# A two-layer network with a dense expert layer on one Trainium2 core: read-back activations in buffers of their own, and 104 instead of 96 expert columns multiplied ahead in the second layer

## Chip, cores and metric

One core of one Trainium2 chip runs the whole program, all in float32 with matrix products split in two or three parts. The metric is the device time of one execution in microseconds (us). Engines are named as in the profile: PE (matmul), PEld (PE's weight load), DVE, ACT, POOL, and SP, whose queue issues every DMA spoken of here.

## The reference, cut to what matters

Two layers over 256 context tokens and 256 latent tokens; the second layer needs the latent tokens alone. Each layer is a mixer (convolution, mLSTM and attention heads side by side) and then an expert layer with 16384 experts. The mixer is not touched by the change. The expert layer is

```python
def one(t):
    q = (t @ wq).reshape(TOKEN_BLOCK, PEER_HEADS, 2, PEER_DK // 2)
    s = jnp.einsum("thpd,hpnd->thpn", q, sub_keys).astype(jnp.float32)
    st, it = lax.top_k(s, PEER_TOPK)
    ...
    e = jnp.take_along_axis(cidx, pos, axis=-1)
    g = jax.nn.softmax(best, axis=-1)
    u = jnp.take(eu, e, axis=0)
    act = jax.nn.gelu(jnp.einsum("thkd,td->thk", u, t).astype(jnp.float32), approximate=False)
    return jnp.einsum("thk,thkd->td", (g * act).astype(ev.dtype), jnp.take(ev, e, axis=0))
```

Each of the 8 heads of a token picks 16 experts by product keys, weighs them with a softmax, and adds up `g * gelu(u . t) * v` over the chosen ones.

## The kernel before, in words

The kernel does the expert layer densely: it multiplies all 16384 experts with all tokens, and a gate matrix G that is zero for experts that were not chosen picks out the right ones. The experts lie in 128 columns `j` of 128 experts each. Layer 0 has n = 512 tokens and layer 1 has n = 256, so one 128x512 tile of activations holds one column in layer 0 and two columns in layer 1 (`per` = 1 and 2).

The expert layer of each layer (`peer`, L896) has two passes.

The **early pass** multiplies columns with the `u` weights (`inner`, L874): load `u`, split each half into a rounded part `uh` (ACT, L869) and a rest `ul` (L870, on POOL here), 24 matmuls (L887 to L889), gelu into a tile `ga` (L893), and a store of that tile to a DRAM buffer `act` (L916). These columns are interleaved with the routing: a top-k phase, and then `spread` (L806), which writes G. One step of `spread` takes four tokens: one-hot tiles on DVE (L824, L832) and ACT (L829, L830), four matmuls L836, two reductions L838 on DVE; every eight steps a 2 MB store of G (L841). The constants `RATE` say how many columns are put in per routing step, `MORE` how many between the two phases, and `NPRE` how many of the 128 columns are multiplied in the early pass at all (128 in layer 0, 96 in layer 1).

The **value pass** (`outer`, L940) then goes over all columns two at a time. `weights` (L946) loads a 1 MB piece `g` of G for every four columns (L954), reads the stored activations back from `act` (L960), multiplies the two on DVE (L966), and splits the product into `wh` (ACT, L969) and `wl` (DVE, L970). `values` (L975) loads the column's `v` (512 KB, L977) and splits both halves into `vh` (ACT, L869) and `vl` (DVE, L870). `second` multiplies: per token tile and half one matmul each of L992, L993 and L994, 24 per column in layer 0 and 12 in layer 1, each 512 wide. The columns that the early pass left (32 in layer 1) get their `u` matmuls here, interleaved with the others (L1042), with their `ul` on DVE. Beside the value pass of layer 0 runs `side`: the modulation vectors for later use, 56 loads `wa` of 512 KB (L193) with two DVE operations `wtr` each (L196), behind one load and sigmoid of the condition vector `cb` (L181 to L185).

The read-back tile of L959 is named `ga` and rotates in the same three buffers of the pool `expu` as the gelu output of L892. The pools are opened and closed in turn on the same memory; a tile in a pool that lies where an earlier pool lay waits until that one is done with. The framework's scheduler turns the loops into one fixed instruction order per engine, from these buffer counts and its own durations; the engines then wait for one another by semaphores.

Of the kernel before, what the change touches and what calls it, by code (L numbers as in the profile page):

```python
# [7 lines left out]
F32 = mybir.dt.float32  # L8
# [15 lines left out]
SPLIT = 3072.0  # L24
TG = 32
TT = 512
NPRE = (128, 96)
RATE = (((1, 3), (5, 8)), ((1, 2), (1, 1)))
UB = (5, 8)
UR = (2, 4)  # L30
VB = (5, 6)
VR = (2, 3)
SPREAD = (('ap', 'as', 'ap', 'ds'), ('as', 'ds'))
LAG = (16, 4)
HB = 4
# [14 lines left out]
class Net:  # L50
# [653 lines left out]
    def route(self, l, h, c0, Gd):  # L704
# [101 lines left out]
        def spread(tt, sT, ni, sg):  # L806

            iota = self.iotap[:, None, :].to_broadcast([128, 4, 128])
            for gq in range(128 // TG):
                stg = R("stg", [128, 128, TG])  # L810
                for t4 in range(0, TG, 4):
                    kind = SPREAD[l][(gq * TG + t4) // 4 % len(SPREAD[l])]
                    t = slice(gq * TG + t4, gq * TG + t4 + 4)
# [82 lines left out]
    def peer(self, l, P, h, c0, npre, side):  # L896
# [9 lines left out]
        with ExitStack() as rs:  # L906
# [13 lines left out]
            for phase in self.route(l, h, c0, Gd):  # L920
# [4 lines left out]
                k += 1  # L925
                a, b = RATE[l][phase]
                if k * a // b > (k - 1) * a // b:
# [12 lines left out]
    def outer(self, l, P, h, c0, npre, Gd, Ad, pool, X, S, side):  # L940
# [9 lines left out]
        def weights(n2):  # L950

            if n2 % 2 == 0:
                st["g"] = X.tile([128, n // TG, 4, TG], F32, name="g", tag="g")
                nc.sync.dma_start(st["g"], Gd[:, :, 2 * n2:2 * n2 + 4, :])  # L954
            r = []
            for m in range(2 // per):
                bank = n2 * (2 // per) + m
                if bank * per < npre:
                    a = pool.tile([128, 512], F32, name="ga", tag="ga", bufs=3)  # L959
                    nc.sync.dma_start(a, Ad[bank])  # L960
                else:
                    a = st.pop(("a", bank))
                j4 = (bank * per) % 4
                av = a.rearrange("p (j a b) -> p j a b", j=per, b=TG)
                g = st["g"][:, :, j4:j4 + per, :].rearrange("p a j b -> p j a b")
                nc.vector.tensor_mul(av, av, g)  # L966
                wh = X.tile([128, 512], F32R, name="wh", tag="wh", bufs=2 * (2 // per))
                wl = X.tile([128, 512], F32R, name="wl", tag="wl", bufs=2 * (2 // per))
                nc.scalar.activation(wh, a, AF.Copy)  # L969
                nc.vector.tensor_sub(wl, a, wh)  # L970
                for k in range(per):
                    r.append((wh[:, k * n:(k + 1) * n], wl[:, k * n:(k + 1) * n]))
            st["w", n2] = r

        def values(j):  # L975
            v = X.tile([128, D], F32, name="v", tag="v", bufs=VR[l])
            nc.sync.dma_start(v, V[:, j, :])  # L977
            return self.usplit(v, "v", X, VB[l], nc.vector)
# [68 lines left out]
        for k in range(65):  # L1047
            if k == 64:
                for _ in side:
                    pass  # L1050
                self.log_exp(self.gelu)
            if k < 64:
                n2 = seq[k]
                for j in (2 * n2, 2 * n2 + 1):
                    if j >= npre:
                        a = self.inner(l, h, c0, j, per, pool, S, nc.vector)
                        if a is not None:
                            st["a", j // per] = a
                weights(n2)
                next(side, None)  # L1060
            if k:
                second(seq[k - 1])
            next(side, None)


    def run(self):
# [4 lines left out]
        for l in range(DEPTH):  # L1071
# [14 lines left out]
            def side():  # L1086
                if l == 0:
                    cb = self.condition()
                    yield
                    for k, (ll, w) in enumerate([(0, 5)] + [(1, w) for w in range(6)]):  # L1090
                        yield from self.ada(ll, P[ll], w, cb, self.I["ada_t"][k])
            self.peer(l, P[l], h, c0, NPRE[l], side())

# [84 lines left out]
```

## Time and profile before

| what | value |
|---|---|
| time, median of 3 runs | 3087.41 us (3082.68 to 3088.37) |
| profiled execution, its time and its span | 3078.09 us and 3076.4 us |
| share of the span: PE, DVE, ACT, POOL | 95%, 68%, 46%, 35% |
| layer 0: early pass, value pass | about 454 to 1230 us, 1235 to 1972 us |
| layer 1: spread phase | about 2391 to 2612 us |
| layer 1: value pass | about 2629 to 3060 us |

The span runs from the first to the last instruction of the profiled execution; 1.7 us of its time lie outside. A share over the whole span mixes stages with different limits, so the rows below come from single stages. "Idle before" is the time that an engine stood still ahead of an instruction, with the instruction or transfer that ended it.

### The profile page before, as it was taken

What the parts mean: (1) busy time and instruction counts of PE and PEld (TensorE: products, weight loads), DVE (VectorE), ACT (ScalarE), POOL (GpSimd) and SP (SyncE); (2) the same over time, 40 slices, a digit from 0 to 9 for tenths busy, and PEclk for the clock granted to TensorE, in tenths of its full rate; (3) what the DMA queues carried; (4) which work ended last, traced back from release to release, by engine and by line L of the source; (5) the groups of instructions that cost most, each with busy time, mean ns of one, the idle gap of its engine ahead of it and who ended that gap; (6) DMA issues with size and microseconds to landing.
All of it is one profiled execution on the core that took longest, in us unless ns stands there. A gap on an engine that the chain in (4) does not pass through costs nothing.

```text
span 3076.4 us, 43429 instructions
## 1 busy us (share of the span) xinstructions
PE 2923.6 (95%) x14930; PEld 2407.8 (78%) x14930; DVE 2088.7 (68%) x4556; ACT 1428.0 (46%) x2865; POOL 1064.0 (35%) x871
## 2 busy tenths in 40 slices
PE   7899989999999999999999999888999998999998
PEld 4476578888888888777777777777689998788887
DVE  7987637875666664666666665586659889666665
ACT  4335443345666655332232233345455665455554
POOL 4334245566666664000000000153478874000000
PEclk9999999999999999999999999999999999999999
DMA  6511124345555557766766766221255876988864
GB/s 227 176 51 56 41 79 136 126 139 187 187 205 184 204 184 250 236 226 222 235 222 216 233 226 199 81 76 62 68 180 174 273 264 229 304 278 263 264 222 141
DMA packets 256717, 563.53 MB, mean 183 GB/s; under 512 B 18208, under 2 KB 119072, under 8 KB 253296
## 3 DMA queue, kind: packets, MB, share of 16 engines
q1 hardware_dynamic: 255776, 558.32, 54.0%
q8 instruction: 118, 1.93, 0.3%
q0 software_dynamic: 720, 2.43, 0.2%
q14 instruction: 103, 0.84, 0.1%
HBM read 463.16 MB, written 97.52 MB: 182 GB/s over the span
## 4 chain that ended last, share of the span: by engine, by line
PE 57%; DMA 14%; DVE 12%; issue 2%; ACT 2%; POOL 1%; SPq 0%; DVEq 0%; ACTq 0%; POOLq 0%
DMA ga<-act 11%; PE h L887 10%; PE h L888 10%; PE h L889 10%; PE acc L993 6%; PE acc L994 5%; PE acc L992 5%; PE f L836 3%; DVE vl L870 2%; DVE wl L970 1%; DVE cy L491 1%; PE f L333 1%; DMA u<-in_peer_u 1%; PE f L334 1%; PE f L335 1%
## 5 line engine op out<-in xcount | busy, mean ns | idle before, releaser
L870 POOL TENSOR_TENSOR ul<-u,uh 128x512 fp32r<-128x512 f32 x448 | 590.8, 1331 | 333.9 <-ACT uh L869 320.0
L887 PE MATMUL h<-hh,uh 128*128 128x512 f32 (+1 forms) x2048 | 693.4, 339 | 2.6 <-ACT ga L893 1.4
L889 PE MATMUL h<-hh,ul 128*128 128x512 f32 (+1 forms) x2048 | 690.5, 337 | 5.2 <-POOL ul L870 5.2
L888 PE MATMUL h<-hl,uh 128*128 128x512 f32 (+1 forms) x2048 | 691.0, 337 | 0.0
L993 PE MATMUL acc<-vl,wh 128*128 128x512 f32 x1536 | 609.4, 397 | 21.2 <-DVE vl L870 19.1
L869 ACT ACTIVATE vh<-v 128x512 fp32r<-128x512 f32 x512 | 305.6, 626 | 660.2 <-DMA v<-in_peer_v 520.8
L992 PE MATMUL acc<-vh,wh 128*128 128x512 f32 x1536 | 599.6, 390 | 6.5 <-ACT wh L969 4.5
L994 PE MATMUL acc<-vh,wl 128*128 128x512 f32 x1536 | 599.9, 391 | 0.2
L869 ACT ACTIVATE uh<-u 128x512 fp32r<-128x512 f32 x512 | 319.4, 629 | 487.1 <-PE h L888 362.6
L870 DVE TENSOR_TENSOR vl<-v,vh 128x512 fp32r<-128x512 f32 x512 | 343.9, 686 | 179.5 <-ACT vh L869 178.7
L889 PEld LDWEIGHTS h<-hh,ul 128*128 128x128 f32 x2048 | 390.7, 191 | 46.4 <-POOL ul L870 5.6
L887 PEld LDWEIGHTS h<-hh,uh 128*128 128x128 f32 x2048 | 391.1, 191 | 43.6 <-ACT ga L893 2.8
L888 PEld LDWEIGHTS h<-hl,uh 128*128 128x128 f32 x2048 | 391.0, 191 | 37.2
L838 DVE TENSOR_REDUCE rt_stg<-f 128x256 f32<-128x512 f32 x384 | 244.8, 686 | 224.3 <-PE f L836 223.5
L993 PEld LDWEIGHTS acc<-vl,wh 128*128 128x128 f32 x1536 | 288.5, 188 | 113.0 <-DVE vl L870 55.5
L992 PEld LDWEIGHTS acc<-vh,wh 128*128 128x128 f32 x1536 | 288.8, 188 | 68.4 <-ACT wh L969 4.9
L994 PEld LDWEIGHTS acc<-vh,wl 128*128 128x128 f32 x1536 | 288.9, 188 | 58.9 <-DVE wl L970 1.6
L241 POOL TENSOR_TENSOR wlo<-wt,whi 128x512 fp32r<-128x512 f32 x164 | 240.7, 1479 | 247.7 <-ACT whi L240 221.7
L966 DVE TENSOR_TENSOR ga<-ga,g 128x512 f32<-128x512 f32 x192 | 131.8, 691 | 217.7 <-DMA ga<-act 201.3
L398 POOL MEMSET up<- 128x60 f32 (+1 forms) x2 | 0.3, 148 | 765.4 <-PE acc L1014 765.4
L824 DVE SCALAR_TENSOR_TENSOR rt_oh_g<-iotap,rt_sT,rt_sg 128x256 fp32r<-128x256 f32 x512 | 213.2, 474 | 0.1
L240 ACT ACTIVATE whi<-wt 128x512 fp32r<-128x512 f32 x164 | 100.5, 627 | 162.4 <-PE f L320 71.2
(317 smaller groups left out, 4277.5 us busy)
## 6 DMA issues: line engine op xcount, KB each, us to landing
u<-in_peer_u SPq DMA_DIRECT2D x256, 512.0 KB, 3.9
v<-in_peer_v SPq DMA_DIRECT2D x256, 512.0 KB, 4.7
G<-rt_stg SPq DMA_DIRECT2D x24, 2048.0 KB, 7.1
act<-ga SPq DMA_DIRECT2D x176, 256.0 KB, 2.9
ga<-act SPq DMA_DIRECT2D x176, 256.0 KB, 4.6
g<-G SPq DMA_DIRECT2D x32, 1024.0 KB, 6.0
wa<-in_ada_t SPq DMA_DIRECT2D x56, 512.0 KB, 5.6
w<-in_ada_w SPq DMA_DIRECT2D x20, 1024.0 KB, 6.3
```

The costliest lines, as they stand in the source:

```text
L241: nc.gpsimd.tensor_sub(lo, raw, hi)
L824: nc.vector.scalar_tensor_tensor(og[:, k], self.iotap[:, None, :].to_broadcast([128, 2, 128]), sT[:, 1, c:c + 1], sg[:, c, :, None].bitcas ...
L838: nc.vector.tensor_reduce(stg[:, :, t4 + k2:t4 + k2 + 2].rearrange("p j t -> p t j"), pg.rearrange("p (t x j) -> p t j x", t=2, x=2), axis ...
L869: nc.scalar.activation(hi, raw[:, k * 512:(k + 1) * 512], AF.Copy)
L870: lo_eng.tensor_sub(lo, raw[:, k * 512:(k + 1) * 512], hi)
L887: nc.tensor.matmul(o, uh, hh[:, c, c0:], start=c == 0, stop=False)
L888: nc.tensor.matmul(o, uh, hl[:, c, c0:], start=False, stop=False)
L889: nc.tensor.matmul(o, ul, hh[:, c, c0:], start=False, stop=c == NB - 1)
L966: nc.vector.tensor_mul(av, av, g)
L992: nc.tensor.matmul(A, wh[:, t], vh, start=s0, stop=False)
L993: nc.tensor.matmul(A, wh[:, t], vl, start=False, stop=False)
L994: nc.tensor.matmul(A, wl[:, t], vh, start=False, stop=s1)
```

## The change

The read-back gets a tile `gb` of its own, in the pool `X` of the value pass, with six buffers in layer 0 and four in layer 1; the three `ga` buffers stay for the gelu output and for the end of the layer. In layer 1, 104 columns are multiplied in the early pass, and nine are put in per eight spread steps where it was one per step; 24 columns are left to the value pass. All lines behind the constants move by one, so L960 becomes L961 and so on.

```diff
-NPRE = (128, 96)
-RATE = (((1, 3), (5, 8)), ((1, 2), (1, 1)))
+NPRE = (128, 104)
+RATE = (((1, 3), (5, 8)), ((1, 2), (9, 8)))
 UB = (5, 8)
 UR = (2, 4)
 VB = (5, 6)
 VR = (2, 3)
+AB = (6, 4)
...
                 if bank * per < npre:
-                    a = pool.tile([128, 512], F32, name="ga", tag="ga", bufs=3)
+                    a = X.tile([128, 512], F32, name="gb", tag="gb", bufs=AB[l])
                     nc.sync.dma_start(a, Ad[bank])
```

How the fixed order moves, at three places. The number behind a name tells one tile from the next.

**The steady part of layer 0's value pass, on DVE.** Before, from the split `wl_13380` on (`ga_13547` uses the buffer that `wl_13380` reads last, `ga_13554` the one that `wl_13463` reads last):

```order
L970 TENSOR_TENSOR wl_13380<-ga_13376,wh_13379 128x512
L196 SCALAR_TENSOR_TENSOR wtr_13383,red_13008<-wa_13365,cb_11572 128x1024
L196 SCALAR_TENSOR_TENSOR wtr_13455,red_13008<-wa_13453,cb_11572 128x1024
L870 TENSOR_TENSOR vl_13478<-v_13475,vh_13477 128x512
L966 TENSOR_TENSOR ga_13547<-ga_13547,g_13457 128x512
L870 TENSOR_TENSOR vl_13482<-v_13475,vh_13481 128x512
L970 TENSOR_TENSOR wl_13463<-ga_13459,wh_13462 128x512
L870 TENSOR_TENSOR vl_13512<-v_13509,vh_13511 128x512
L966 TENSOR_TENSOR ga_13554<-ga_13554,g_13457 128x512
L870 TENSOR_TENSOR vl_13516<-v_13509,vh_13515 128x512
```

The same place with the change (`gb_14086` uses the buffer that `wl_13824` reads last, `gb_14093` the one that `wl_13831` reads last):

```order
L971 TENSOR_TENSOR wl_13824<-gb_13820,wh_13823 128x512
L871 TENSOR_TENSOR vl_13873<-v_13870,vh_13872 128x512
L967 TENSOR_TENSOR gb_14086<-gb_14086,g_13996 128x512
L871 TENSOR_TENSOR vl_13877<-v_13870,vh_13876 128x512
L971 TENSOR_TENSOR wl_13831<-gb_13827,wh_13830 128x512
L197 SCALAR_TENSOR_TENSOR wtr_13834,red_13725<-wa_13814,cb_11572 128x1024
L197 SCALAR_TENSOR_TENSOR wtr_13906,red_13725<-wa_13904,cb_11572 128x1024
L871 TENSOR_TENSOR vl_13927<-v_13924,vh_13926 128x512
L967 TENSOR_TENSOR gb_14093<-gb_14093,g_13996 128x512
L871 TENSOR_TENSOR vl_13931<-v_13924,vh_13930 128x512
```

The multiplication by `g` now stands six tiles ahead of its own split instead of about three, and still two to six DVE rows behind the split that gives its buffer free, with the second `vl` half of a column right behind it.

**The same stretch on SP.** Before, between two loads of `g`:

```order
L954 DMA g_13635<-G0_3117 128x16x128
L977 DMA v_13419<-in_peer_v 128x1024
L193 DMA wa_13453<-in_ada_t 128x1024
L960 DMA ga_13459<-act0_3118 128x512
L960 DMA ga_13466<-act0_3118 128x512
L977 DMA v_13475<-in_peer_v 128x1024
L977 DMA v_13509<-in_peer_v 128x1024
L960 DMA ga_13547<-act0_3118 128x512
L193 DMA wa_13543<-in_ada_t 128x1024
L977 DMA v_13563<-in_peer_v 128x1024
L960 DMA ga_13554<-act0_3118 128x512
L954 DMA g_13818<-G0_3117 128x16x128
```

With the change:

```order
L955 DMA g_13635<-G0_3117 128x16x128
L978 DMA v_13297<-in_peer_v 128x1024
L961 DMA gb_13459<-act0_3118 128x512
L978 DMA v_13331<-in_peer_v 128x1024
L961 DMA gb_13466<-act0_3118 128x512
L194 DMA wa_13365<-in_ada_t 128x1024
L978 DMA v_13385<-in_peer_v 128x1024
L961 DMA gb_13547<-act0_3118 128x512
L978 DMA v_13419<-in_peer_v 128x1024
L961 DMA gb_13554<-act0_3118 128x512
L194 DMA wa_13453<-in_ada_t 128x1024
L955 DMA g_13818<-G0_3117 128x16x128
```

The transfers are the same ones; now every read-back stands right behind a `v`, and two of each follow the `g`.

**The end of layer 1's spread phase, on PE.** Before:

```order
L888 MATMUL h<-hl,uh 128x256
L836 MATMUL f<-rt_oh_g,rt_oh_i 128x256 x4
L889 MATMUL h<-hh,ul 128x256
L836 MATMUL f<-rt_oh_g,rt_oh_i 128x256 x16
L887 MATMUL h<-hh,uh 128x256
L888 MATMUL h<-hl,uh 128x256
L889 MATMUL h<-hh,ul 128x256
```

With the change:

```order
L889 MATMUL h<-hl,uh 128x256
L890 MATMUL h<-hh,ul 128x256
L837 MATMUL f<-rt_oh_g,rt_oh_i 128x256 x4
L888 MATMUL h<-hh,uh 128x256
L889 MATMUL h<-hl,uh 128x256
L890 MATMUL h<-hh,ul 128x256
```

Before, the early pass's last `u` matmul is followed by 16 spread matmuls, and then by the 96 `u` matmuls of four late columns before the first value matmul. Now the last four spread matmuls stand with `u` matmuls around them, and 153 `u` matmuls (57 of early columns, 96 of late ones) follow them before the first value matmul.

## Rows read from the trace of the kernel before

**Rows 1.** Busy time by stretch: PE, PEld, DVE, ACT, POOL us (instructions), PE clock, DMA share, GB/s.
```profile
1235.00:1972.00 737.00, 716.23 (x3050) 567.01 (x3051) 446.38 (x739) 215.32 (x382) 0.00 (x0) 1.00 0.65 216
...
2395.00:2598.00 203.00, 203.00 (x1671) 200.95 (x1670) 182.25 (x376) 138.04 (x299) 149.16 (x116) 1.00 0.77 269
...
2598.00:2630.00 32.00, 20.38 (x123) 18.31 (x122) 25.37 (x47) 10.47 (x21) 0.00 (x0) 0.79 0.60 214
...
2700.00:2800.00 100.00, 100.00 (x533) 86.68 (x532) 66.08 (x104) 53.33 (x93) 0.00 (x0) 1.00 0.84 276
```

**Rows 2.** PE in order of time at layer 0's change of pass: start, us, what, [idle before].
```profile
1219.61 0.39 PE L888 MATMUL h<-hl,uh 128*128 128x512 f32 x1
...
1230.04 0.39 PE L889 MATMUL h<-hh,ul 128*128 128x512 f32 x1
1234.95 0.53 PE L992 MATMUL acc<-vh,wh 128*128 128x512 f32 x1 [4.52 <-ACT wh L969]
```

**Rows 3.** Waits, 1400 to 1800 us: engine, line, waited for, total us, times, longest us.
```profile
DVE ga L966 <- DMA ga<-act: 89.9, 51, 4.3
...
PE acc L993 <- DVE vl L870: 11.0, 25, 1.0
```

**Rows 4.** DVE in order of time, layer 0 value pass: one cycle of four columns.
```profile
1606.41 0.69 DVE L870 TENSOR_TENSOR vl<-v,vh 128x512 fp32r<-128x512 f32 x1 [3.26 <-ACT vh L869]
1607.62 1.44 DVE L966 TENSOR_TENSOR ga<-ga,g 128x512 f32<-128x512 f32 x2 [0.52 <-DMA ga<-act]
...
1610.18 1.22 DVE L196 SCALAR_TENSOR_TENSOR wtr<-wa,cb 128x1024 bf16<-128x1024 f32 x1
...
1611.33 1.22 DVE L196 SCALAR_TENSOR_TENSOR wtr<-wa,cb 128x1024 bf16<-128x1024 f32 x1
...
1614.30 0.69 DVE L966 TENSOR_TENSOR ga<-ga,g 128x512 f32<-128x512 f32 x1 [1.14 <-DMA ga<-act]
...
1615.51 0.69 DVE L970 TENSOR_TENSOR wl<-ga,wh 128x512 fp32r<-128x512 f32 x1
1616.11 0.68 DVE L870 TENSOR_TENSOR vl<-v,vh 128x512 fp32r<-128x512 f32 x1
1620.21 0.69 DVE L966 TENSOR_TENSOR ga<-ga,g 128x512 f32<-128x512 f32 x1 [3.42 <-DMA ga<-act]
```

**Rows 5.** SP's DMA issues of the same stretch: start, us, what.
```profile
1597.80 0.53 SPq L954 DMA_DIRECT2D g<-G  x1
1598.43 1.57 SPq L977 DMA_DIRECT2D v<-in_peer_v  x1
...
1616.22 0.33 SPq L960 DMA_DIRECT2D ga<-act  x1
1620.93 0.53 SPq L954 DMA_DIRECT2D g<-G  x1
```

**Rows 6.** Line L977, 1235 to 1960 us: landing of the 124 loads of `v`.
```profile
DMA to landing us min/median/max: 3.5/4.5/8.1
```

**Rows 7.** SP at layer 0's change of pass: the first read-back.
```profile
1228.48 0.33 SPq L960 DMA_DIRECT2D ga<-act  x1
```

**Rows 8.** PE from the end of layer 1's spread phase to its first value matmul.
```profile
2598.73 0.28 PE L889 MATMUL h<-hh,ul 128*128 128x256 f32 x1
...
2604.27 1.62 PE L836 MATMUL f<-rt_oh_g,rt_oh_i 128*128 128x256 f32 x6 [3.07 <-DVE rt_oh_i L832]
...
2613.13 0.58 PE L887 MATMUL h<-hh,uh 128*128 128x256 f32 x1 [1.12 <-DVE rt_stg L838]
...
2628.91 0.49 PE L992 MATMUL acc<-vh,wh 128*128 128x512 f32 x1 [2.02 <-ACT vh L869]
```

**Rows 9.** SP of the same stretch.
```profile
2613.10 0.32 SPq L841 DMA_DIRECT2D G<-rt_stg  x1
...
2621.68 0.53 SPq L954 DMA_DIRECT2D g<-G  x1
2622.26 1.12 SPq L977 DMA_DIRECT2D v<-in_peer_v  x2
```

## The prediction

> **What bounds the kernel now.** I read the busy time by stretch first, since a share over the whole span mixes stages. Layer 0's value pass takes 737 us [rows 1]. PE's own pace is in the rows of the early pass, which has no gaps: the starts at 1219.61 and 1230.04 are 46 matmuls apart, 0.2267 us each [rows 2]. The value pass of layer 0 has 128 x 24 = 3072 matmuls of the same width, so PE needs 696.5 us and stands about 40.5 us, in small gaps, at a full clock. In layer 1's spread phase PE is busy for 203.00 of 203 us [rows 1], and so it is in the value pass of layer 1 (100.00 of 100): there PE itself is the bound. Between the two lies a stretch where it is not: 20.38 of 32 us busy, at a granted clock of 0.79 [rows 1].
>
> The waits say what the gaps of layer 0 are. PE waits for `vl` (11.0 us in 400, and more is hidden in pipelining), and DVE, which makes `vl`, waits 89.9 us for read-backs [rows 3]. The reader should see the order in it: DVE runs its list in order, so a multiplication that waits for its read-back holds up the `vl` behind it. One cycle of four columns shows all four stops: 3.26 us for `vh` (that is, for a `v`), 0.52, 1.14 and 3.42 us for read-backs [rows 4]. The cycle lasts 23.13 us (from one `g` to the next, 1597.80 to 1620.93 [rows 5]) where PE needs 96 x 0.2267 = 21.77. The last stop is plain: `wl` at 1615.51 frees a buffer, its load is issued at 1616.22 [rows 5], and the multiplication that needs it starts at 1620.21, 3.99 us after the issue.
>
> **Part 1, own buffers, steady part of layer 0.** Six buffers instead of three suggest that this stop goes. The order says otherwise: the scheduler used the room to put the multiplication earlier, six tiles ahead, and again two DVE rows behind the split that frees its buffer (`wl_13824`, one `vl`, then `gb_14086`). The load cannot be issued before that split has run, so the landing of about 4 us is waited for again, less one `vl`. I follow the new cycle with prices from the rows: a `vl`, multiplication or `wl` takes 0.60 us from start to start (1615.51 to 1616.11), a `wtr` 1.15 (1610.18 to 1611.33) [rows 4]. A cycle has 16 of the first and 4 of the second: 14.2 us. The stops now: 3.4 us at the multiplication two rows behind its `wl`, as before; 1.2 at the one with one `vl` and two `wtr` more between; 1.3 at the second of the pair behind a `g`; and 3.5 at the first `vl` whose `v` is issued right behind a `g`. Such a `v` was issued at 1598.43 [rows 5] and its `vl` started at 1606.41 [rows 4], 8.0 us later, where 4.5 is the median landing of a `v` [rows 6]. Together 9.4 us, so 23.6 us a cycle. The same walk through the old order gives 23.3, where the trace has 23.13, so I trust the difference more than the level: 0.25 us in each of 32 cycles, **+8 us**. The ends are far apart: -40.5 if every stop is covered and PE sets the pace, +22 if each cycle gets 0.7 us longer, the other stops keeping their size while the 0.52 becomes the 1.2 that its neighbours have. I stay near the middle since the two long stops, 3.26 and 3.42 us, keep their causes.
>
> **Part 2, layer 0's change of pass.** PE ends the early pass with the matmul of 1230.04 and starts the value pass at 1234.95 [rows 2]: 4.9 us, 4.7 more than one matmul, waiting for `wh`, for a read-back that was issued only at 1228.48 [rows 7] because gelu outputs still held the three buffers. With own buffers four read-backs stand on SP ahead of the last two stores and `v` loads. **-4.7 us**; the upper end is 0, if `v` or the first splits take the gap. The freed memory also lets the condition load and two `wa` loads move hundreds of us forward, beside the query weights; I cost this at nothing, as only one transfer of 1 MB is new there. If it is not covered, it is at most what a `g` does to the `v` behind it, 8.0 less 4.5 or 3.5 us, either way, once.
>
> **Part 3, eight more columns ahead in layer 1.** The early pass's last `u` matmul but for late columns is at 2598.73 [rows 8]. The 16 spread matmuls that follow wait for their one-hot tiles, 3.07 us at a time, until PE reaches the late columns at 2613.13; their 96 matmuls run at a lowered clock, and the first value matmul is at 2628.91 [rows 8]. So PE does 16 + 96 narrow matmuls in 30.2 us. One costs 203.00/1671 = 0.12 us [rows 1].
>
> With the change, a spread step carries 9/8 x 24 = 27 `u` matmuls and 4 of its own: 31 x 0.12 = 3.72 us, against 28 x 0.12 = 3.36. DVE is busy 182.25 of 203 us and POOL 149.16 [rows 1]; DVE has as much to do per step as before, in a longer step, and POOL the same per column, so PE stays the bound and the spread no longer runs dry. From 2598.73 on I add what PE still has to do: 8 x 24 = 192 new matmuls less the 57 that come after the spread, and the 16 spread matmuls, 151 x 0.12 = 18.1 us. The last reduction is then at about 2617. Then 153 matmuls (18.4 us) end at about 2635.5, 6.6 us later than 2628.91. The value pass is shorter by the 192 matmuls, 23.0 us, and there PE is always busy, so all of it is gained. **-16.4 us.**
>
> These 18.4 us have to cover the chain from the last reduction: its store of G at 2613.10, the load of `g` at 2621.68, `v` at 2622.26 [rows 9], value matmul at 2628.91: 15.8 us. Now one store and two read-backs stand between `g` and `v`, 0.3 to 0.5 us each, so about 17.3. It is just covered; if another 4.5 us of landing come in, a `v`'s median [rows 6], some 3 us are left standing, and -13 is the upper end. It can hardly be more than -16.4, as all that PE still has to do is counted. The 16 `ul` of the eight columns go from DVE to POOL, and four stores and four read-backs are added in a stage where PE is the bound: nothing.
>
> **Sum.** +8 - 4.7 + 0 - 16.4 = -13.1 on the profiled execution's 3078.1 us: 3065. That execution was 9.3 us faster than the median of the runs, so the forecast for a median is 3087.4 - 13.1 = **3074 us**.
>
> **Rivals.**
> *The ring opens.* The stops are at most 4.3 us long [rows 3] and the tiles are multiplied six ahead, so irregular landings could be absorbed and PE could be the bound: 40.5 us gone, no +8, 3074 - 8 - 40.5 = 3026 us. Against it stands the two-row distance in the new order. The Trainium skill ("Perfetto Trace Analysis", Optimization Strategy) reads a gap that repeats on the engine that should be saturated as a possible sign of too few buffers. By that rule this would be the outcome; the trace bears it out in so far as the 3.42 us stop does follow a buffer's release. Chance 0.16.
>
> *The bunch behind `g` lands later, and the kernel is slower.* Two `v` and two read-backs now follow each `g` on SP, 1.5 MB; before, the `wa` and the read-backs lay between. If the two long stops grow by 0.75 us each, a cycle grows by 1.5 us more, 48 us over 32: 3122. It decides early: all gain is lost when the cycle is longer by 13.1/32 = 0.4 us than I have it, two stops of 0.2 us. For it speaks that a `v` can land as late as 8.1 us [rows 6]; against it that total traffic is unchanged and the DMA share is 0.65 [rows 1]. The Trainium skill ("DMA: Bandwidth & Descriptors", Latency and other measured facts) gives the memory's access latency as 0.2 us on average and 2 us under high load; no row here separates that part of a landing. Chance 0.14.
>
> *The tail is not filled.* The scheduler's order is fixed, but if the one-hot tiles still come late, for instance because ACT serves `uh` first, PE waits as before and nothing or a few us of part 3 are gained: 3087.4 + 8 - 4.7 is 3091, with 3 us of it 3088, no change. For it speaks the 3.07 us at a time [rows 8]; against it that DVE has 0.36 us more per step. Chance 0.14.
>
> **How the numbers follow.** The forecast's own case has 0.56. Its range comes from its terms: ring -8 to +22 (openings by a fifth of the 40.5 count to it), tail -16.4 to -13, change of pass 0 to -4.7, condition -3.5 to +3.5: 3055 to 3100. The range for 8 in 10 reaches from 3026, the ring's opening, to 3100, and leaves out most of the slower case. A measurement of this kernel can tell about 0.2%, 6.2 us, from no change. Within the own case some 0.48 lies below 3081 and 0.08 within the bound; the open ring is faster; the unfilled tail is 0.12 no change and 0.02 faster; the slower case is slower. Faster 0.66, same 0.20, slower 0.14.
>
> **What would show it.** In the changed kernel's profile: PE about 825 matmuls per 200 us in layer 0's value pass (882 if the ring opens, under 800 if the bunch is late); on DVE still some 90 us in 400 of waits of the multiplication for `gb`, with stops of over 3 us behind a `wl`; no PE gap of 4 us at the change of pass; and in layer 1 PE busy without a gap, at a full clock, from the spread phase into the value pass. The prediction is wrong if the cycle differs from 23.1 us by over 0.5, or if PE stands over 5 us between the last spread matmul and the first value matmul.

## The result, and the profile after

The changed kernel takes 3066.0 us (median of 4 runs, 3058.5 to 3072.0), the kernel before beside it 3086.9. The ratio is 0.9937, interval 0.9922 to 0.9953: 19.4 us less, or 14.5 to 24.1 (the two medians lie 20.8 apart), where 13.1 less were forecast (3074 on 3087.4). The profiled execution, 3072.0 us with a span of 3070.0, is the longest of the four.

Busy time by stretch of the changed kernel (PE, PEld, DVE, ACT, POOL us and instructions, PE clock, DMA share, GB/s): layer 0's value pass, layer 1's spread phase, its end, and a part of the value pass of layer 1, beside [rows 1]:

```profile
1235.00:1989.00 754.00, 727.92 (x3139) 580.07 (x3138) 445.46 (x760) 223.00 (x396) 0.00 (x0) 1.00 0.64 210
...
2399.00:2609.00 210.00, 209.74 (x1729) 207.78 (x1729) 188.11 (x387) 143.21 (x309) 162.30 (x127) 1.00 0.77 270
...
2610.00:2641.00 31.00, 29.32 (x241) 28.88 (x241) 19.60 (x35) 16.75 (x31) 9.53 (x8) 1.00 0.81 281
...
2700.00:2800.00 100.00, 99.40 (x477) 82.22 (x476) 68.46 (x109) 53.39 (x95) 0.00 (x0) 1.00 0.89 300
```

The hole at the end of the spread phase has gone: PE is busy for 29.32 of 31 us at a full clock there, where it was 20.38 of 32 at 0.79. In layer 0's value pass PE still stands: it is busy for 727.92 of 754 us. (The stretch of [rows 1] ends at 1972 us, with 3050 of the pass's 3072 matmuls; the last one starts at 1985.2. The landmarks further down take the whole pass.) The waits between 1400 and 1800 us (engine, line, waited for, total us, times, longest), beside [rows 3]:

```profile
DVE gb L967 <- DMA gb<-act: 95.3, 51, 5.2
DVE vl L871 <- ACT vh L870: 59.9, 17, 4.0
...
PE acc L994 <- DVE vl L871: 17.3, 26, 2.0
```

The wait for read-backs, 89.9 us before, is 95.3 us with twice as many buffers, in 51 waits as before. One cycle on DVE in order of time (start, us, what, [idle before]), beside [rows 4]:

```profile
1614.61 0.69 DVE L871 TENSOR_TENSOR vl<-v,vh 128x512 fp32r<-128x512 f32 x1 [3.98 <-ACT vh L870]
1615.21 0.68 DVE L967 TENSOR_TENSOR gb<-gb,g 128x512 f32<-128x512 f32 x1
1616.71 0.69 DVE L967 TENSOR_TENSOR gb<-gb,g 128x512 f32<-128x512 f32 x1 [0.81 <-DMA gb<-act]
...
1617.92 0.68 DVE L971 TENSOR_TENSOR wl<-gb,wh 128x512 fp32r<-128x512 f32 x1
...
1622.43 0.69 DVE L967 TENSOR_TENSOR gb<-gb,g 128x512 f32<-128x512 f32 x1 [3.23 <-DMA gb<-act]
...
1629.31 0.69 DVE L967 TENSOR_TENSOR gb<-gb,g 128x512 f32<-128x512 f32 x1 [2.08 <-DMA gb<-act]
```

and SP's issues of the same stretch, beside [rows 5]:

```profile
1605.35 0.53 SPq L955 DMA_DIRECT2D g<-G  x1
1605.98 1.61 SPq L978 DMA_DIRECT2D v<-in_peer_v  x1
...
1618.63 0.33 SPq L961 DMA_DIRECT2D gb<-act  x1
...
1630.03 0.53 SPq L955 DMA_DIRECT2D g<-G  x1
```

The four stops are 3.98, 0.81, 3.23 and 2.08 us. The third shows why: the split at 1617.92 frees the buffer, the load goes out at 1618.63, and the multiplication, two DVE rows behind the split, waits for it until 1622.43. From `g` to `g` this cycle lasts 24.68 us, and so it is a long one: by PE's matmuls, the median of all 31 whole cycles is 23.27 us, as before, and the mean behind the first four is 23.61 us, where it was 23.38.

At layer 0's change of pass PE stands 1.8 us instead of 4.9 (beside [rows 2]):

```profile
1232.65 0.39 PE L890 MATMUL h<-hh,ul 128*128 128x512 f32 x1
1234.48 0.50 PE L993 MATMUL acc<-vh,wh 128*128 128x512 f32 x1 [1.43 <-ACT ga L894]
```

and at the end of layer 1's spread phase (PE, beside [rows 8]; then SP, beside [rows 9]):

```profile
2619.86 0.64 PE L837 MATMUL f<-rt_oh_g,rt_oh_i 128*128 128x256 f32 x4
...
2632.81 0.39 PE L888 MATMUL h<-hh,uh 128*128 128x256 f32 x1 [1.15 <-ACT ga L894]
...
2640.79 0.73 PE L993 MATMUL acc<-vh,wh 128*128 128x512 f32 x2 [0.53 <-ACT vh L870]
```

```profile
2622.10 0.38 SPq L842 DMA_DIRECT2D G<-rt_stg  x1
...
2632.07 0.53 SPq L955 DMA_DIRECT2D g<-G  x1
2632.78 0.53 SPq L917 DMA_DIRECT2D act<-ga  x1
2633.36 0.94 SPq L961 DMA_DIRECT2D gb<-act  x2
2634.34 0.98 SPq L978 DMA_DIRECT2D v<-in_peer_v  x2
```

PE goes on with `u` matmuls behind the last spread matmuls. It has one gap of 1.15 us at 2632.81 and one of 0.53 before the first value matmul, at 2640.79, 8.7 us after the load of `g`.

Where the time went, by landmarks on PE (us):

| stretch | before | changed | forecast of the difference |
|---|---|---|---|
| 6 us gap in the query stage to first `u` matmul, layer 0 | 52.1 | 47.6 | 0 |
| change of pass in layer 0 | 4.9 | 1.8 | -4.7 |
| value pass of layer 0 and its end | 750.2 | 754.3 | +8 |
| layer 1, first `u` matmul to last value matmul | 786.1 | 772.0 | -16.4 |

The rest of the two profiled executions differs by some 11 us the other way, in stretches that the change does not touch: 7.0 us ahead of the query stage and 3.8 in layer 1's mixer. A second profile of the changed kernel (below, on another chip) has them at 0.8 and 1.0 us, so they belong to the single execution.

### The profile page after: what moved, and what is told of

It is laid out like the page before. It is cut to its first block, busy times and chain, and to the rows that moved or that the text cites. A ratio compares the mean times of both kernels' runs of the same rounds, so it can differ in the third digit from the quotient of the medians.

```text
span 3070.0 us, 43388 instructions
## 1 busy us (share of the span) xinstructions
PE 2925.5 (95%) x14930; PEld 2411.4 (79%) x14930; DVE 2074.5 (68%) x4540; ACT 1424.7 (46%) x2864; POOL 1088.6 (35%) x887
## 4 chain that ended last, share of the span: by engine, by line
PE 60%; DMA 12%; DVE 11%; issue 2%; ACT 1%; POOL 1%; SPq 0%; DVEq 0%; ACTq 0%; POOLq 0%
PE h L888 10%; PE h L889 10%; PE h L890 10%; DMA gb<-act 10%; PE acc L994 6%; PE acc L995 6%; PE acc L993 6%; PE f L837 3%; DVE vl L871 2%; DVE wl L971 2%; DVE cy L492 1%; PE f L334 1%; PE f L335 1%; PE f L336 1%; DMA v<-in_peer_v 1%
## 5 line engine op out<-in xcount | busy, mean ns | idle before, releaser
L871 POOL TENSOR_TENSOR ul<-u,uh 128x512 fp32r<-128x512 f32 x464 | 611.2, 1326 | 335.6 <-ACT uh L870 320.4
L967 DVE TENSOR_TENSOR gb<-gb,g 128x512 f32<-128x512 f32 x180 | 126.0, 702 | 263.0 <-DMA gb<-act 238.7
```

The lines of the kernel that those rows point to most:

```text
L871: lo_eng.tensor_sub(lo, raw[:, k * 512:(k + 1) * 512], hi)
```

## The experiments

Eleven runs, of eight new kernels and of three once more, in three lots; the kernels of a lot share their runs of the kernel before (3093.8, 3083.9 and 3083.8 us). Ratios are to these. The first lot is the column counts alone, the buffers alone for the first time, and the held multiplication with six and with three own buffers; it ran on one chip, the other two lots on another.

### The two parts of the change alone

The column counts alone:

```diff
-NPRE = (128, 96)
-RATE = (((1, 3), (5, 8)), ((1, 2), (1, 1)))
+NPRE = (128, 104)
+RATE = (((1, 3), (5, 8)), ((1, 2), (9, 8)))
```

> The kernel before with the new column counts alone: 104 columns ahead in layer 1, nine per eight spread steps; read-backs stay in the three shared ga buffers. My theory: the whole gain of the change sits here, about 14 us (the changed kernel's profile has 771.9 us from layer 1's first expert matmul to its last value matmul, the kernel before 786.1), so a ratio near 0.9955 and some 3073 us; layer 0 as before, 4.9 us of gap at the change of pass included. Rival (the buffers are what carries the gain, in layer 1 too): under 5 us of gain, ratio above 0.998, since the read-backs of four more columns queue for the shared buffers at the handover.

3081.6 us, ratio 0.9962 (0.9947 to 0.9976). Layer 1 takes 770.0 us, 16.0 less than before, with the read-backs still in the shared buffers; layer 0 keeps its 5.2 us at the change of pass. The rival is out: the gain in layer 1 is the columns'. But layer 0's value pass, in the same order as before, took 764.3 us in this profile.

The buffers alone (the changed kernel with the two constants set back):

> The changed kernel with the old column counts (96 columns, one per step): own buffers alone, six in layer 0 and four in layer 1. My theory: no gain to speak of, the value pass of layer 0 at 750 to 757 us as in the changed kernel (754.3, before 750.2), 3 us less at the change of pass, the hole of about 30 us with 112 narrow matmuls at the end of layer 1's spread still there; ratio 0.998 to 1.003. Rival (buffers carry the gain): ratio at 0.995 or below.

3081.1 us, ratio 0.9953 (0.9939 to 0.9967), a miss for my expectation: the buffers gain some 14 us. The hole in layer 1 is still there (785.5 us), and layer 0's value pass took 763.6 us. To tell kernel from chip I ran three kernels once more, together, on the other chip:

> The kernel before, unchanged, for a profile of it on the chip of the other kernels and for the size of the noise: ratio 0.9985 to 1.0015. If the value pass of layer 0 is near 765 us here (as in the kernel with the column counts alone, whose layer 0 is the same order), then its length varies by some 14 us with the chip or the run, and a single profile cannot show a term of 8 us in it.

> The kernel with own buffers alone, a second time (ratio 0.9953 before). My corrected theory: it gains 9 to 15 us, ratio 0.995 to 0.997: about 4 us in the query stage, 3 us at the change of pass, 1 to 2 us in the first cycles, and within 5 us of nothing in the steady cycles. Rival (the steady cycles gained, and the first profile fell on a long one): the value pass of layer 0 over 8 us shorter than that of the repeated kernel before.

> The changed kernel on the chip of the other kernels. If the two parts add up, own buffers (0.9953) and column counts (0.9962) give 0.9915; if they overlap in layer 1's handover, 0.993 to 0.994 as measured on the first chip (0.9937).

The kernel before repeats itself: 3084.9 us, ratio 0.9998 (0.9987 to 1.0008), value pass 751.6 us. The buffers alone: 3073.4 us, 0.9960 (0.9945 to 0.9976), as the corrected theory has it, value pass 751.3. The changed kernel: 3068.3 us, 0.9946 (0.9931 to 0.9961), value pass 755.5. The wait for read-backs in the same 400 us, first in the repeated kernel before, then with buffers alone:

```profile
DVE ga L966 <- DMA ga<-act: 90.8, 51, 5.0
```

```profile
DVE gb L967 <- DMA gb<-act: 93.2, 51, 5.0
```

So the steady cycles gain nothing. Chip by chip, old order against six buffers, the value pass takes 750.2 and 754.3 us in the first pair, 764.3 and 763.6 on the chip of the first lot, and 751.6 against 751.3 and 755.5 on the other. The long passes go with the first lot, not with the number of buffers. What the buffers do gain is seen in two places: the change of pass (4.5 to 5.2 us before, 1.1 to 2.6 now) and the query stage of layer 0 (51.8 to 52.1 us in every profile with the old buffers, 47.9 and 48.1 here). That makes about 7 us; the rest of their 12 to 14 us I could not place, since the profiled executions of both kernels with buffers alone were among the longer ones of their runs. Nor do the parts add up: together they would give 0.9915, and the changed kernel has 0.9937 and 0.9946. It is not layer 1, where the buffers alone gain next to nothing (785.5 and 785.8 us against 786.1 and 786.0); why the sum falls short is not shown.

### What bounds the cycle: the place of the multiplication

In the changed kernel, the multiplication of layer 0 is held on DVE behind what precedes it in the program:

```diff
-                nc.vector.tensor_mul(av, av, g)
+                mul = nc.vector.tensor_mul(av, av, g)
+                if l == 0:
+                    self.tc.keep_in_program_order(mul)
```

> The changed kernel, and in layer 0 the multiplication by g is held on DVE behind what precedes it in the program, so that only the load runs ahead: it then stands three rows before its own split, and its buffer's release lies several columns back. My theory (in the changed kernel DVE waits for a landing because the multiplication stands right behind the release of its buffer): the 95 us in 400 of waits of the multiplication for its read-back go to under 15, PE sets the pace at 21.8 us per four columns, layer 0's value pass drops from 754 to 705 to 720 us, and the time to 3020 to 3035 us, ratio near 0.98. Rival (landings and DMA load bound the cycle, wherever the multiplication stands): the wait moves to vh and v, the value pass stays above 740 us and the ratio at 0.993.

3010.0 us, ratio 0.9741 (0.9720 to 0.9763), more than expected; on this chip the old order's cycles were the long ones (764.3 us). The value pass of layer 0 is down to 704.4 us, and every cycle takes 21.8 us. Busy time and waits of this kernel, 1400 to 1800 us, and DVE in order of time:

```profile
1400.00:1800.00 400.00, 400.00 (x1767) 331.31 (x1766) 268.49 (x449) 124.18 (x221) 0.00 (x0) 1.00 0.76 244
```

```profile
ACT vh L870 <- PE acc L997: 273.2, 74, 3.8
DVE vl L871 <- ACT vh L870: 131.7, 77, 2.9
ACT vh L870 <- DMA v<-in_peer_v: 4.2, 5, 1.5
```

```profile
1611.72 1.22 DVE L197 SCALAR_TENSOR_TENSOR wtr<-wa,cb 128x1024 bf16<-128x1024 f32 x1
...
1612.87 0.69 DVE L967 TENSOR_TENSOR gb<-gb,g 128x512 f32<-128x512 f32 x1
...
1615.42 0.68 DVE L973 TENSOR_TENSOR wl<-gb,wh 128x512 fp32r<-128x512 f32 x1
1616.02 0.69 DVE L967 TENSOR_TENSOR gb<-gb,g 128x512 f32<-128x512 f32 x1
1616.62 0.69 DVE L871 TENSOR_TENSOR vl<-v,vh 128x512 fp32r<-128x512 f32 x1
1620.25 0.69 DVE L871 TENSOR_TENSOR vl<-v,vh 128x512 fp32r<-128x512 f32 x1 [2.94 <-ACT vh L870]
```

PE is busy for 400.00 of 400 us, no wait for a read-back is left, and what DVE and ACT still wait for is PE (273.2 us). The multiplication now follows straight on a `wtr` or a `wl` with no idle time.

The same with three own buffers (`AB = (3, 4)`):

> As the kernel with the held multiplication, but with three own read-back buffers in layer 0 instead of six. My theory (the place of the multiplication decides, not the number of buffers): within 5 us of the kernel with six, 3022 to 3040 us, the value pass of layer 0 at 705 to 722 us. Rival (depth is what counts): the read-back waits come back, the value pass is above 735 us and the time within 6 us of the changed kernel's.

3016.5 us, ratio 0.9750 (0.9733 to 0.9767), value pass 704.5 us: the cycle needs no more than three. The medians lie 6.5 us apart, a little over the 5 that I expected, and the intervals overlap. (Its query stage takes 52.1 us, see below.)

The kernel before, with this one line held and nothing else:

> The kernel before (three shared ga buffers, 96 columns ahead), and only the multiplication by g in layer 0 held on DVE behind what precedes it in the program. My theory (the place of the multiplication alone sets the cycle): layer 0's value pass falls to 704 to 722 us, with the gap of 5 us at the change of pass and the 3 us one in the query stage still there; some 45 to 60 us less, ratio 0.980 to 0.986. Rival (own buffers are needed for the ring to open): the value pass stays above 735 us, ratio above 0.99.

3038.0 us, ratio 0.9855 (0.9839 to 0.9872), value pass 706.3 us, with a gap of 3.9 us at the change of pass and 51.8 us in the query stage. Busy time, 1400 to 1800 us:

```profile
1400.00:1800.00 400.00, 400.00 (x1767) 331.20 (x1766) 270.10 (x453) 123.83 (x220) 0.00 (x0) 1.00 0.76 241
```

The three shared buffers were enough all along; the order was not. By the trace, the held multiplication stands 9 to 17 DVE rows behind the split that frees its buffer. Holding this one DVE instruction also moves loads on SP: a `v` right behind a `g` lands after 5.0 us in the median here, not after 7.3. So the held kernels change two things at once; in the next one such a `v` still lands after 7.3 us.

With six buffers, one of a cycle's four multiplications stands two DVE rows behind the split that frees its buffer; the others, by the trace, stand four, five and seven behind (the section on the change has two to six for all). With nine (`AB = (9, 4)`, nothing held):

> The changed kernel with nine instead of six own buffers in layer 0, the multiplication not held. By the order its multiplications then stand 3 to 8 DVE rows behind the split that frees their buffer, instead of 2 to 6. My theory (the distance from release to multiplication sets the wait, not the number of buffers as such): about half of the stops go, the value pass of layer 0 at 710 to 735 us, ratio 0.978 to 0.989, behind the held kernel with three buffers (0.975). Rival 1 (depth does nothing): 750 to 765 us, ratio 0.993 to 0.996. Rival 2 (depth alone opens the ring): 704 to 708 us, ratio under 0.977.

3019.2 us, ratio 0.9787 (0.9769 to 0.9804): the ratio within my expectation, but the value pass, 707.9 us, shorter than it, almost as the second rival had it. Its busy time, its wait for read-backs, and two rows of its DVE:

```profile
1400.00:1800.00 400.00, 399.90 (x1764) 330.63 (x1762) 265.95 (x448) 128.54 (x222) 0.00 (x0) 1.00 0.74 242
```

```profile
DVE gb L967 <- DMA gb<-act: 67.1, 25, 3.6
```

```profile
1609.57 0.69 DVE L967 TENSOR_TENSOR gb<-gb,g 128x512 f32<-128x512 f32 x1 [3.17 <-DMA gb<-act]
...
1618.98 1.29 DVE L871 TENSOR_TENSOR vl<-v,vh 128x512 fp32r<-128x512 f32 x2 [3.42 <-ACT vh L870]
```

The waits are fewer, 25 instead of 51, but the rows that I expected, 3 to 8, were wrong. By the trace between 1300 and 1900 us, one multiplication of four still stands two rows behind its release (twice three), and the others 5 to 13. Both long stops are still there: the one at two rows lasts 3.2 us in the median (3.4 with six buffers), and the one for the `v` behind a `g` 3.4 (3.5). What went are the short stops, 1.1 and 0.7 us in the median with six, and that was enough. An estimate from these rows: DVE's work, 14.2 us a cycle by the prediction's sum, and two long stops make 20.8 us, under PE's 21.8; with the four stops of six buffers it is 22.9, over it. (The sum leaves out small gaps; with six, the cycles last 23.6 us in the mean.) So no single stop sets the cycle; what counts is whether DVE's work and all its stops together fit into PE's time. Holding the multiplication removes every stop for a read-back; nine buffers remove just enough.

### Two smaller questions

The sigmoids of the condition vector held at their old place, in the changed kernel:

```diff
-            nc.scalar.activation(sg, cb[:, s], AF.Sigmoid)
+            self.tc.keep_in_program_order(nc.scalar.activation(sg, cb[:, s], AF.Sigmoid))
```

> The changed kernel, with the two sigmoids of the condition vector held on ACT behind what precedes them in the program, so that they and the wa work stand at layer 0's change of pass again. In the query stage ACT still has the third uh behind the query copies. My theory (that swap of one uh is what gave 4 us in the query stage): the time from the 6 us gap to the first expert matmul stays at 47.5 to 48.5 us (52 before). Rival (the early condition work gave it): back to 51 to 52.5 us. Either way the whole lies within 6 us of the changed kernel, ratio 0.992 to 0.9965.

3060.2 us, ratio 0.9919 (0.9905 to 0.9933); the interval touches those of the changed kernel, so that no gain over it is shown. The query stage stays at 47.3 us: the early sigmoids and `wa` loads did not bring the gain there. What else differs is the place of one `uh` on ACT, and on SP the load of `cb`, which still stands early in this run (at 417.73 us). ACT before, with the PE matmul that waits for it, and ACT in the changed kernel:

```profile
428.24 0.63 ACT L869 ACTIVATE uh<-u 128x512 fp32r<-128x512 f32 x1 [2.23 <-DMA u<-in_peer_u]
428.77 0.61 ACT L240 ACTIVATE whi<-wt 128x512 fp32r<-128x512 f32 x1
429.29 1.55 ACT L713 ACTIVATE rt_q<-f 128x512 f32<-128x512 f32 x3
```

```profile
429.92 0.80 PE L333 MATMUL f<-hh,whi 128*128 128x512 f32 x1 [3.02 <-ACT rt_q L713]
```

```profile
432.11 1.14 ACT L241 ACTIVATE whi<-wt 128x512 fp32r<-128x512 f32 x2
433.15 1.55 ACT L714 ACTIVATE rt_q<-f 128x512 f32<-128x512 f32 x3
436.44 0.63 ACT L241 ACTIVATE whi<-wt 128x512 fp32r<-128x512 f32 x1 [1.74 <-DMA wt<-in_peer_wq]
436.98 0.58 ACT L714 ACTIVATE rt_q<-f 128x512 f32<-128x512 f32 x1
437.61 0.63 ACT L870 ACTIVATE uh<-u 128x512 fp32r<-128x512 f32 x1
```

Before, an `uh` that waited 2.23 us for its load stood ahead of the copies `rt_q`, for which PE then waited 3.02 us; now it stands behind them. The kernel with three own buffers has the `uh` ahead of the copies, as before, and there the stage takes 52.1 us. So the place of this one `uh` goes with the time in all thirteen profiles, 51.8 to 52.1 us ahead and 47.3 to 48.1 behind. But so does the load of `cb`, which is early in the same eight profiles and late in the other five; neither was tried by itself, so that the cause is not shown.

The multiplication held in both layers:

> The changed kernel with the multiplication by g held in both layers. Layer 0 as in the kernel with layer 0 held alone: value pass 704 us. In layer 1 PE is the bound and has about 3 us of gaps between 60 and 200 us into its value pass; my theory: 0 to 4 us less than with layer 0 alone, ratio 0.972 to 0.9745. Rival: the held multiplication comes too late for PE in layer 1, whose value pass grows by over 5 us, ratio above 0.976.

3012.2 us, ratio 0.9759 (0.9746 to 0.9773); layer 1 takes 768.8 us, against 769.7 with layer 0 alone held. The ratio lies above the range that I gave. The two ratios come from different lots and their intervals overlap; nothing is gained that can be told.

The version to keep is the changed kernel with the multiplication held in layer 0: some 80 us less than before, four times the gain of the change.

## Why the prediction was right, and where its terms were off

The time lies in the range and near the forecast, with the sign of the likeliest case, but its nearness is partly luck: the four terms were off by 1.6 to 4.5 us in the first pair of profiles, two each way.

*Steady part of layer 0, +8.* The reading of the order was right: a multiplication stands two rows behind its buffer's release, so the landing is waited for again. The forecast stops were 3.5, 1.3, 3.4 and 1.2 us; between 1300 and 1900 us they are 3.5, 0.7, 3.4 and 1.1 in the median (in the old order 3.4, 0.6, 3.4 and 1.1). The held multiplications and the nine buffers show that these stops bound the cycle. The size was nearly right for the cycles, and the whole pass hides it. From the fifth to the 31st cycle, six buffers take 23.61 us in the mean against 23.38 in the first pair, 23.87 against 23.70 on the chip of the first lot, and 23.49, 23.61 and 23.68 against 23.43 on the other: longer each time, by 0.06 to 0.25 us where 0.25 was forecast. (These are single profiles, and 23.49 and 23.61 come from the same order on the same chip.) The part left out is the start: the first four cycles take 87.2 us where they took 89.1 (1 to 5 us less in the other pairs), since six tiles are there before PE needs the first. So the whole pass was 4.1 us longer in the first pair, and from 0.7 shorter to 5.0 longer in the others. The walk through the old order that gave 23.3 us is not written out, and the sign of 825 matmuls per 200 us fits a cycle of 23.3 us, not the forecast 23.6, which gives 814; the profile has 808 and 809. The 40.5 us that an open ring was to gain were 45 when the kernel before had its multiplication held (751.6 to 706.3 us): the 737 us of the prediction hold 3050 matmuls and not 3072.

*Change of pass, -4.7.* Right in kind, too large in size: -3.1 in the first profile, and 1.1 us are left in most of the others, which makes -3.4 to -3.8.

*Query stage, 0, with 3.5 us either way.* This step failed: -4.5 us in the first profile, some -4 in every other with six buffers or more, outside the bound of 3.5. I had priced the transfer that moves there and not looked at what moves on ACT; which of the two brought the gain stays open.

*Layer 1, -16.4.* Right in mechanism and nearly in size: PE stays the bound of the spread phase, and the chain to the first value matmul is covered but for little. The changed kernel took 14.1 and 12.5 us less there in its two profiles, and 14.1 to 17.2 less in the five others that have both parts. The margin of the cover was thin, as written: `g` was loaded 9.97 us after its store was issued, not 8.58, and PE stood 1.15 and 0.53 us.

*The sum.* -13.1 forecast; -19.4 (0.9937) and -16.7 (0.9946) measured. By the landmarks of the first pair it is +4.1 - 3.1 - 4.5 - 14.1 = -17.6: the steady part 3.9 us and the query stage 4.5 better than forecast, the change of pass 1.6 and layer 1 2.3 worse.

*The rivals.* The ring did not open with six buffers. The bunch behind `g` did not cost what its rival had: a `v` behind a `g` landed after 7.3 us in the median, as before. The read-backs did land later, after 5.4 us in the median instead of 4.6, but the cycles grew by no more than 0.25 us, where that rival had 1.5 on top. The rule of the Trainium skill ("Perfetto Trace Analysis", Optimization Strategy), by which a repeating gap can mean too few buffers, would have pointed here to more of them. This case agrees in part: the gap stayed with six (754.3 us) and nearly went with nine (707.9), but with the same three shared buffers it went as well when the order was changed (706.3).

## What to carry to other kernels

Where a scheduler fixes the order, more buffers for a load can be spent on moving its user forward, so that the user again stands right behind the release: look at how many rows lie between the instruction that frees a buffer and the one that waits for the new content, before and after. In this kernel DVE, waiting there, held up every `vl` behind it; holding the consumer back, and letting only the load run ahead, gained 45 us with no buffer added. Add up the work and all the stops of such an engine over one cycle, and compare the sum with the time of the engine that should be the bound: removing the short stops was enough here. And when memory moves, look at every engine's order in the stages around it, not only at the transfers.

## What was not expected

The same order of layer 0's value pass took 750.2 and 751.6 us in two executions and 764.3 in a third, on the chip of the first lot, where six buffers took 763.6 too. On the other chip two executions of the changed order took 751.3 and 755.5. So a cycle closed by landings varied by 4 us from run to run, and by some 10 more with the chip, though one profile of each kernel cannot tell chip from chance. Once PE set the pace, it took 704.4, 704.5 and 704.4 us in three kernels, on both chips. And some 4 us that no line of the diff names went with the places of one ACT instruction and one load, hundreds of us ahead of the code that was changed.
